# Down products of a two-layer encoder's feed-forward blocks by seven block products in place of eight, and their exchange issued by GpSimd, on one Trainium2 core

## The chip, the cores and the metric

The kernel runs on one core of one Trainium2 chip. The metric is the device time of one execution in microseconds, the median of three runs. All arithmetic is in float32, at the accuracy of float32: each operand is split into a high part (a cast to the type fp32r) and a low part (what the cast left), and a product takes three matmuls (high by high, high by low, low by high).

## The reference

Input `x` is 256 rows of 1024. Two layers; each adds half a feed-forward block (FFN), then a token mixer (retention in layer 0, latent attention in layer 1) together with a cross-attention into memory, then half a second FFN. What the change touches is the FFN:

```python
def swiglu(h, w_gu, w_down):            # w_gu 1024 x 5632, w_down 2816 x 1024
    g, u = jnp.split(h @ w_gu, 2, axis=-1)
    return (jax.nn.silu(g) * u) @ w_down
...
x = x + 0.5 * rms_norm(swiglu(rms_norm(x, ng[0]), ffn_w_gu[l, 0], ffn_w_down[l, 0]), ng[1])
```

There are four of them, named (l, j) here: (0,0), (0,1), (1,0), (1,1).

## The kernel before

The 256 rows are two tiles t of 128. The 2816 hidden columns go in eleven chunks c of 256 (`FC`, `NFC`; `C` is 10). For a chunk and a tile `gu(t, c)` multiplies the normed rows (`zh`, `zl`, columns on partitions) with 8 blocks of gate and up weights side by side: 8 x 3 = 24 matmuls of 512 columns into one PSUM bank. `swiglu` (L311, L313) drains that bank: ScalarE makes s, the silu of the gate half, VectorE multiplies the up half with it into `a`. For the down product the hidden columns must lie on the partitions. `turn` (L330) has VectorE transpose `a` in 32 x 32 squares into `aT`; every two chunks `exchange` moves the squares between partition groups into `ag`: four blocks stay in their partitions and are copied by GpSimd (L265), twelve are moved by DMAs of 32 x 256 (L260), which SP issues. `take` splits `ag` into `ah` and `al`. The last chunk goes through TensorE's transposes instead (`tr`).

`down(t, c)` multiplies a tile's 128 x 256 with the chunk's 256 x 1024: two halves i of 512 columns, two blocks b, three matmuls each, 12 in all, into two banks `accs[t]`; `both(c)` does the two tiles, 24. In the loop the order on TensorE, which is written out by hand, is gu(0, c), gu(1, c), both(c - 3): 72 matmuls of 512 columns. The four accumulators hold four of the eight banks, the rest are for gate/up and transposes.

Weights come by SP's DMAs into `raw` (5 buffers). ScalarE casts the high part `wh` (L75), VectorE subtracts it for the low part `wl` (L76), both in pieces of 1024 columns, with 9 buffers each: four pieces for gate/up and two for down a chunk. The other engines' order is the scheduler's, by the order of the program and by `issue_after`; SP's exchange transfers stand between weight loads in steps (`between`, `moved`). `extra` is other work placed into an FFN's turns: rotary tables, and the memory's preparation for the next mixer. `post` scales the FFN's result, adds it to x, and `pre` prepares the next stage; rsqrt is GpSimd's (L159).

Of the kernel before, what the change touches and what calls it, by code (L numbers as in the profile page):

```python
# [10 lines left out]
F32 = mybir.dt.float32  # L11
# [7 lines left out]
P = 128  # L19
# [3 lines left out]
FC = 256  # L23
# [8 lines left out]
def kernel(ctx, tc, x, mem, positions, norm_gains, ffn_w_gu, ffn_w_down, w_o,  # L32
# [46 lines left out]
    def load_raw(src, cols):  # L79
        with behind(*moved):  # L80
            return load_now(src, cols)

    def load_now(src, cols):
# [10 lines left out]
        if between:  # L94
            between[0][0] -= 1
            if between[0][0] < 0:
                with behind_weights():
                    moved[:] = [between[0][1].pop(0)()]
                if not between[0][1]:
                    between.pop(0)  # L100
# [3 lines left out]
    between, moved = [], []  # L104
# [123 lines left out]
    def post(t, accs, gain, half, next_gain, hook=None):  # L228
# [5 lines left out]
        ends = next_gain is None  # L234
        if not ends:
            scaled(0)
            scaled(1)
# [18 lines left out]
    def exchange(b, g, skip, n):  # L256


        def move(i, q):
            return nc.sync.dma_start(out=g[q * 32:(q + 1) * 32, i * 256:(i + 1) * 256],  # L260
                                     in_=b[i * 32:(i + 1) * 32, q * 256:(q + 1) * 256]).ins
        pairs = []
        for i in range(4):
            sl = slice(i * 32, (i + 1) * 32)
            G.tensor_copy(out=g[sl, i * 256:(i + 1) * 256], in_=b[sl, i * 256:(i + 1) * 256])  # L265
            pairs += [(i, q) for q in range(4) if q != i]
        steps = [lambda p=pairs[k:k + n]: [move(*x) for x in p][-1] for k in range(0, 12, n)]
        if n == 12:
            steps[0]()
        else:  # L270
            between.append([skip, steps])
# [6 lines left out]
    def ffn(l, j, zs, gains, extra=(), first=None):  # L278
        wgu, wd = ffn_w_gu[l, j], ffn_w_down[l, j]
        gu_w, d_w, act, at, pair = {}, {}, {}, {}, {}  # L280
        accs = [[None, None], [None, None]]
        extra = dict(extra)
# [25 lines left out]
        def swiglu(t, c):  # L308
# [4 lines left out]
            a_ins = V.scalar_tensor_tensor(out=a, in0=p[:, FC:2 * FC], scalar=z.r, in1=s,  # L313
                                           op0=ALU.mult, op1=ALU.mult).ins
# [9 lines left out]
        def turn(t, c):  # L324
# [938 lines left out]
```

## Time and profile before

| | before |
|---|---|
| time, median of 3 runs | 963.52 us (962.76 to 964.04) |
| the profiled execution, its own time | 961.57 us |
| its span, first to last instruction | 959.8 us |
| busy: TensorE, VectorE, ScalarE, GpSimd | 947.4, 627.1, 516.7, 78.3 us |
| instructions | 13112 |
| DMA moved | 188.96 MB, 197 GB/s over the span |

The span is of one profiled execution; the time of an execution is 1.8 us longer than its span. Busy time counts the instructions' own durations, and neighbours on an engine overlap a little, so an engine's step from one start to the next can be shorter than its instruction.

### The profile page before, as it was taken

What the parts mean: (1) busy time and instruction counts of PE and PEld (TensorE: products, weight loads), DVE (VectorE), ACT (ScalarE), POOL (GpSimd) and SP (SyncE); (2) the same over time, 40 slices, a digit from 0 to 9 for tenths busy, and PEclk for the clock granted to TensorE, in tenths of its full rate; (3) what the DMA queues carried; (4) which work ended last, traced back from release to release, by engine and by line L of the source; (5) the groups of instructions that cost most, each with busy time, mean ns of one, the idle gap of its engine ahead of it and who ended that gap; (6) DMA issues with size and microseconds to landing.
All of it is one profiled execution on the core that took longest, in us unless ns stands there. A gap on an engine that the chain in (4) does not pass through costs nothing.

```text
span 959.8 us, 13112 instructions
## 1 busy us (share of the span) xinstructions
PE 947.4 (99%) x4503; PEld 788.6 (82%) x4503; DVE 627.1 (65%) x1000; ACT 516.7 (54%) x873; POOL 78.3 (8%) x122
## 2 busy tenths in 40 slices
PE   8999999999999999999999999999999999999997
PEld 7778888898888888888887888888897888878885
DVE  6587657677886846665668456676766884557562
ACT  7455555466655635454546444554658763345451
POOL 0011001020000201000001000001020010100010
PEclk9999999999999999999999999999999999999999
DMA  9488867483745437686745676687551645656851
GB/s 296 126 289 268 254 191 247 151 295 110 211 162 163 132 104 255 198 260 197 249 153 180 209 229 216 210 287 228 169 169 45 220 132 180 198 193 204 271 177 44
DMA packets 148692, 188.96 MB, mean 197 GB/s; under 512 B 13321, under 2 KB 131089, under 8 KB 148625
## 3 DMA queue, kind: packets, MB, share of 16 engines
q1 hardware_dynamic: 148608, 188.12, 60.7%
q8 instruction: 35, 0.57, 0.2%
q14 instruction: 33, 0.26, 0.1%
q10 hardware_dynamic: 16, 0.00, 0.0%
HBM read 179.16 MB, written 1.05 MB: 188 GB/s over the span
## 4 chain that ended last, share of the span: by engine, by line
PE 79%; DMA 6%; SPq 5%; DVE 5%; issue 2%; ACT 2%; POOL 0%; DVEq 0%; POOLq 0%; ACTq 0%
PE bank L156 25%; PE bank L155 25%; PE bank L154 25%; DMA raw<-in_ffn_w_gu_dram 5%; PE bank L184 3%; SPq L91 2%; DVE wl L76 2%; SPq L260 2%; ACT wh L75 1%; PE bank L540 1%; PE bank L572 1%; PE bank L792 1%; PE bank L778 1%; DVE x L248 0%; DVE a L313 0%
## 5 line engine op out<-in xcount | busy, mean ns | idle before, releaser
L76 DVE TENSOR_TENSOR wl<-raw,wh 128x1024 fp32r<-128x1024 f32 (+1 forms) x320 | 383.6, 1213 | 197.3 <-ACT wh L75 193.9
L75 ACT CAST wh<-raw 128x1024 fp32r<-128x1024 f32 (+1 forms) x320 | 331.6, 1047 | 274.0 <-DMA raw<-in_ffn_w_down_dram 109.2
L154 PE MATMUL bank<-wh,zh 128*128 128x512 f32 (+2 forms) x944 | 364.4, 386 | 0.0
L155 PE MATMUL bank<-wl,zh 128*128 128x512 f32 (+2 forms) x944 | 360.7, 382 | 1.3 <-DVE wl L76 1.2
L156 PE MATMUL bank<-wh,zl 128*128 128x512 f32 (+2 forms) x944 | 360.7, 382 | 0.4 <-DVE zl L76 0.4
L155 PEld LDWEIGHTS bank<-wl,zh 128*128 128x128 f32 x944 | 177.7, 188 | 35.4 <-DVE wl L76 2.0
L156 PEld LDWEIGHTS bank<-wh,zl 128*128 128x128 f32 x944 | 177.5, 188 | 34.9 <-DVE zl L76 1.0
L154 PEld LDWEIGHTS bank<-wh,zh 128*128 128x128 f32 x944 | 177.6, 188 | 33.5 <-issue 0.7
L156 PE MATMUL bank<-wh,al 128*128 128x512 f32 x352 | 137.8, 391 | 1.2 <-DVE al L76 1.2
L154 PE MATMUL bank<-wh,ah 128*128 128x512 f32 x352 | 138.2, 393 | 0.1
L155 PE MATMUL bank<-wl,ah 128*128 128x512 f32 x352 | 137.2, 390 | 0.0
L265 POOL COPY ag<-aT 32x256 f32<-32x256 f32 x80 | 40.4, 505 | 501.6 <-DVE aT L330 422.2
L156 PEld LDWEIGHTS bank<-wh,al 128*128 128x128 f32 x352 | 66.1, 188 | 16.8 <-DVE al L76 3.1
L154 PEld LDWEIGHTS bank<-wh,ah 128*128 128x128 f32 x352 | 66.1, 188 | 13.7 <-ACT ah L75 0.5
L155 PEld LDWEIGHTS bank<-wl,ah 128*128 128x128 f32 x352 | 66.1, 188 | 13.4
L311 ACT ACTIVATE s<-bank,rstd 128x256 f32<-128x256 f32 x88 | 41.3, 469 | 51.3 <-PE bank L156 48.4
L313 DVE SCALAR_TENSOR_TENSOR a<-bank,rstd,s 128x256 f32<-128x256 f32 x88 | 42.1, 478 | 32.0 <-ACT s L311 31.7
L168 ACT ACTIVATE junk<-bank 128x512 bf16<-128x512 f32 x24 | 14.4, 599 | 43.0 <-DVE y L233 30.6
L330 DVE STREAM_TRANSPOSE aT<-a 128x256 f32<-128x256 f32 x80 | 35.3, 441 | 1.5
L76 DVE TENSOR_TENSOR al<-ag,ah 128x256 fp32r<-128x256 f32 x80 | 29.7, 417 | 5.7 <-ACT ah L75 5.7
L75 ACT CAST zh<-bank 128x512 fp32r<-128x512 f32 (+2 forms) x54 | 23.0, 455 | 17.6 <-PE bank L184 10.4
L233 DVE TENSOR_TENSOR y<-bank,gpost 128x512 f32<-128x512 f32 x24 | 16.2, 685 | 23.6 <-PE bank L156 19.5
(159 smaller groups left out, 551.2 us busy)
## 6 DMA issues: line engine op xcount, KB each, us to landing
raw<-in_ffn_w_gu_dram SPq DMA_DIRECT2D x352, 256.0 KB, 4.5
raw<-in_ffn_w_down_dram SPq DMA_DIRECT2D x88, 512.0 KB, 4.6
raw<-in_ret_w_in_dram SPq DMA_DIRECT2D x48, 256.0 KB, 4.0
raw<-in_w_o_dram SPq DMA_DIRECT2D x16, 512.0 KB, 4.5
ag<-aT SPq DMA_DIRECT2D x240, 32.0 KB, 2.3
raw<-in_mem_w_kv_dram SPq DMA_DIRECT2D x8, 512.0 KB, 5.3
gpost<-in_norm_gains_dram SPq DMA_DIRECT2D x6, 512.0 KB, 5.9
gpre<-in_norm_gains_dram SPq DMA_DIRECT2D x5, 512.0 KB, 6.3
```

The source lines that it names most:

```text
L75: ins = S.copy(out=hi, in_=src).ins
L76: V.tensor_tensor(out=lo, in0=src, in1=hi.bitcast(F32), op=ALU.subtract)
L91: last_load[0] = nc.sync.dma_start(out=dst[:, k], in_=src[:, k]).ins
L154: T.matmul(out=dst, lhsT=ah, rhs=bh, start=start, stop=False)
L155: T.matmul(out=dst, lhsT=ah, rhs=bl, start=False, stop=False)
L156: T.matmul(out=dst, lhsT=al, rhs=bh, start=False, stop=stop)
L184: T.transpose(out=tp[:s.shape[1], j * P:(j + 1) * P], in_=s, identity=ident)
L260: return nc.sync.dma_start(out=g[q * 32:(q + 1) * 32, i * 256:(i + 1) * 256], in_=b[i * 32:(i + 1) * 32, q * 256:(q + 1) * 256]).ins
L265: G.tensor_copy(out=g[sl, i * 256:(i + 1) * 256], in_=b[sl, i * 256:(i + 1) * 256])
L311: s_ins = S.activation(out=s, in_=p[:, 0:FC], func=AF.Silu, scale=z.r).ins
L313: a_ins = V.scalar_tensor_tensor(out=a, in0=p[:, FC:2 * FC], scalar=z.r, in1=s, op0=ALU.mult, op1=ALU.mult).ins
L330: V.transpose(out=b.rearrange("p (q u t b x) -> p u t q b x", q=4, u=2, t=2, b=2)[:, c % 2, t], in_=act.pop((t, c)).rearrange("p (b q x) - ...
```

## The change

A chunk's down product over both tiles is a 256 x 256 by 256 x 1024 product, seen as 2 x 2 blocks: tile by hidden block b, and hidden block b by column half i. In the first `fast` chunks of an FFN it is made by the Strassen-Winograd form: seven block products of sums and differences in place of eight, each of three matmuls as before. `fast` is 5 in (0,0) and (1,0), and 8 in (0,1) and (1,1).

- Weights (`load_fast`): three blocks x, T's and y's sources come into a tile `wB` and the fourth into `w21`; VectorE makes y (1024 columns), T (512) and w21 (512) as differences between splits.
- Activations (`take_fast`): four sums of 128 columns, and splits of 256, 128 and 512 columns in place of two of 256.
- Order on TensorE: `half(c - 4, 1)`, ten matmuls, behind gu(0, c), and `half(c - 3, 0)`, eleven, behind gu(1, c). The seven products (`prod`) accumulate over the fast chunks in seven banks, which leaves one for gate/up.
- The drain: in these turns ScalarE makes s and also u, the scaled up half; VectorE multiplies the two.
- After chunk fast - 1 `combine` adds the products up; three banks go on as accumulators, and `post` adds the four `sums` to them (two additions of 512 columns for a tile).
- Exchange: GpSimd issues the twelve DMAs, then makes its four copies; the code that put them between SP's loads is gone.
- Tables move to behind gu(1, 1) and gu(1, 2), the memory's steps from turns 6, 7, 8 to 7, 8, 9; one buffer more of `t2`, one fewer of `k1`.

```diff
+        if sums[0] is not None:
+            for a, b in zip(accs, sums):
+                V.tensor_tensor(out=b, in0=a, in1=b, op=ALU.add)
+            accs = sums
...
-    def exchange(b, g, skip, n):
-
-
-        def move(i, q):
-            return nc.sync.dma_start(out=g[q * 32:(q + 1) * 32, i * 256:(i + 1) * 256],
-                                     in_=b[i * 32:(i + 1) * 32, q * 256:(q + 1) * 256]).ins
-        pairs = []
+    def exchange(b, g):
+        for i in range(4):
+            sl = slice(i * 32, (i + 1) * 32)
+            for q in range(4):
+                if q != i:
+                    G.dma_start(out=g[q * 32:(q + 1) * 32, i * 256:(i + 1) * 256], in_=b[sl, q * 256:(q + 1) * 256])
         for i in range(4):
             sl = slice(i * 32, (i + 1) * 32)
             G.tensor_copy(out=g[sl, i * 256:(i + 1) * 256], in_=b[sl, i * 256:(i + 1) * 256])
-            pairs += [(i, q) for q in range(4) if q != i]
-        steps = [lambda p=pairs[k:k + n]: [move(*x) for x in p][-1] for k in range(0, 12, n)]
-        if n == 12:
-            steps[0]()
-        else:
-            between.append([skip, steps])
...
+        def load_fast(c):
+            w = wk.tile([P, 1536], F32, name="wB", tag="A", bufs=2)
+            w21 = esm("wB21")
+            nc.sync.dma_start(out=w[:, 0:1024], in_=block(c, 0, 0, 2))
+            nc.sync.dma_start(out=w[:, 1024:1536], in_=block(c, 1, 1))
+            last_load[0] = nc.sync.dma_start(out=w21, in_=block(c, 1, 0)).ins
+            three = w.rearrange("p (a n) -> p a n", a=3)
+            xh, xl, yh, yl, vh, vl = (wp.tile([P, 1024], F32R, name=n, tag=n)
+                                      for n in ("wh", "wl", "wh", "wl", "wh", "wl"))
+            th, tl = (wk.tile([P, 512], F32R, name=n, tag="e", bufs=5) for n in ("wTh", "wTl"))
+            lo, hi = slice(0, 512), slice(512, 1024)
+            two = lambda a: a.rearrange("p (a n) -> p a n", a=2)
+            split(three[:, 0:3:2], two(xh), two(xl))
+            V.tensor_tensor(out=w[:, 0:1024], in0=w[:, 512:1536], in1=w[:, 0:1024], op=ALU.subtract)
+            split(w[:, 0:1024], yh, yl)
+            split(w21, vh[:, lo], vl[:, lo])
+            V.tensor_tensor(out=three[:, 2], in0=three[:, 2], in1=three[:, 0], op=ALU.subtract)
+            split(three[:, 2], th, tl)
+            V.tensor_tensor(out=w21, in0=w21, in1=three[:, 2], op=ALU.subtract)
+            split(w21, vh[:, hi], vl[:, hi])
+            d_w[c] = [(xh[:, lo], xl[:, lo]), (xh[:, hi], xl[:, hi]), (yh[:, lo], yl[:, lo]), (yh[:, hi], yl[:, hi]),
+                      (vh[:, lo], vl[:, lo]), (vh[:, hi], vl[:, hi]), (th, tl)]
+        def take_fast(c):
+            g = pair.pop(c)
+            A = [[g.rearrange("p (i u t b x) -> p u t b i x", i=4, u=2, t=2, b=2)[:, c % 2, t, b]
+                  for b in range(2)] for t in range(2)]
+            q = lambda a, k, n=1: a[:, k * P:(k + n) * P].rearrange("p (i x) -> p i x", i=4)
+            ah, al = t2("ah", 512, F32R), t2("al", 512, F32R)
+            sr, sh, sl = t2("sr"), t2("sh", 512, F32R), t2("sl", 512, F32R)
+            V.tensor_tensor(out=q(sr, 0), in0=A[1][0], in1=A[1][1], op=ALU.add)
+            V.tensor_tensor(out=q(sr, 1), in0=q(sr, 0), in1=A[0][0], op=ALU.subtract)
+            V.tensor_tensor(out=q(sr, 2), in0=A[0][0], in1=A[1][0], op=ALU.subtract)
+            V.tensor_tensor(out=q(sr, 3), in0=A[0][1], in1=q(sr, 1), op=ALU.subtract)
+            split(g.rearrange("p (i u t b x) -> p u t b i x", i=4, u=2, t=2, b=2)[:, c % 2, 0],
+                  ah[:, 0:FC].rearrange("p (b i x) -> p b i x", i=4, b=2),
+                  al[:, 0:FC].rearrange("p (b i x) -> p b i x", i=4, b=2))
+            split(A[1][1], q(ah, 2), q(al, 2))
+            split(sr, sh, sl)
+            n = lambda k: slice(k * P, (k + 1) * P)
+            a = lambda k: (ah[:, n(k)], al[:, n(k)])
+            z = lambda k: (sh[:, n(k)], sl[:, n(k)])
+            at[c] = [a(0), z(3), z(0), z(2), a(1), a(2), z(1)]
+        def down_fast(c, *ms):
+            if c not in d_w:
+                load_fast(c)
+            if c == 0 and 0 in ms:
+                prod.extend(bank() for _ in range(7))
+                accs[0][:] = prod[4], prod[1]
+                accs[1][0] = prod[5]
+            for m in ms:
+                p, x = divmod(m, 3)
+                (ah, al), (bh, bl) = at[c][p], d_w[c][p]
+                own = p in (1, 4, 5)
+                T.matmul(out=prod[p], lhsT=al if x == 2 else ah, rhs=bl if x == 1 else bh,
+                         start=c == 0 and x == 0, stop=x == 2 and c == fast - 1 and not own)
+        def combine():
+            m1, m5, m7, m6 = prod[0], prod[2], prod[3], prod[6]
+            c1, u, v, w = esm("c1"), esm("u"), esm("v"), esm("w")
+            S.copy(out=c1, in_=m1)
+            add = lambda o, a, b: V.tensor_tensor(out=o, in0=a, in1=b, op=ALU.add)
+            add(u, m6, c1)
+            add(v, m5, u)
+            add(u, m7, u)
+            add(w, m5, u)
+            sums[:] = [[c1, v], [u, w]]
...
-            a_ins = V.scalar_tensor_tensor(out=a, in0=p[:, FC:2 * FC], scalar=z.r, in1=s,
-                                           op0=ALU.mult, op1=ALU.mult).ins
+            if 3 < c < fast + 4 and (t, c) != (1, C):
+                u = k1("u")
+                s_ins = S.activation(out=u, in_=p[:, FC:2 * FC], func=AF.Copy, scale=z.r).ins
+                a_ins = V.tensor_tensor(out=a, in0=u, in1=s, op=ALU.mult).ins
+            else:
+                a_ins = V.scalar_tensor_tensor(out=a, in0=p[:, FC:2 * FC], scalar=z.r, in1=s,
+                                               op0=ALU.mult, op1=ALU.mult).ins
...
+        def half(c, h):
+            if 0 <= c < fast:
+                down_fast(c, *(range(11, 21) if h else range(11)))
+                if h and c == fast - 1:
+                    combine()
...
         for c in range(3, C):
             gu(0, c)
+            half(c - 4, 1)
             gu(1, c)
...
-            both(c - 3)
+            if c - 3 < fast:
+                half(c - 3, 0)
+            else:
+                both(c - 3)
         gu(0, C)
-        both(C - 3)
+        half(C - 4, 1)
+        if C - 3 < fast:
+            half(C - 3, 0)
+            half(C - 3, 1)
+        else:
+            both(C - 3)
...
-    zs = ffn(0, 1, zs, lambda: (gpost(0, 5), gpre(1, 0)))
+    zs = ffn(0, 1, zs, lambda: (gpost(0, 5), gpre(1, 0)), fast=8)
```

TensorE, FFN (0,1), with the change: the ten matmuls of a chunk's second half between two runs of 24 gate/up matmuls (zh, zl are the normed rows; ah, al the activations; sh, sl their sums; wTh, wTl the parts of T).

```order
L144 MATMUL bank<-wh,zl 128x512
L342 MATMUL bank<-wh,sl 128x512
L342 MATMUL bank<-wh,ah 128x512
L342 MATMUL bank<-wl,ah 128x512
L342 MATMUL bank<-wh,al 128x512
L342 MATMUL bank<-wh,ah 128x512
L342 MATMUL bank<-wl,ah 128x512
L342 MATMUL bank<-wh,al 128x512
L342 MATMUL bank<-wTh,sh 128x512
L342 MATMUL bank<-wTl,sh 128x512
L342 MATMUL bank<-wTh,sl 128x512
L142 MATMUL bank<-wh,zh 128x512
```

Before, gate/up of both tiles came without a break, and then the 24 down matmuls in one run; now eleven and ten stand behind one tile's gate/up each.

VectorE, FFN (0,1), before: what stands between the transposes of two tiles in the loop.

```order
L330 STREAM_TRANSPOSE aT<-a 128x4x64
L76 TENSOR_TENSOR wl<-raw,wh 128x1024 x6
L313 SCALAR_TENSOR_TENSOR a<-bank,rstd,s 128x256
L76 TENSOR_TENSOR al<-ag,ah 128x256 x2
L330 STREAM_TRANSPOSE aT<-a 128x4x64
```

The same place with the change.

```order
L76 TENSOR_TENSOR wl<-wB,wh 128x1024
L382 TENSOR_TENSOR a<-u,s 128x256
L297 TENSOR_TENSOR wB<-wB 128x1024
L401 STREAM_TRANSPOSE aT<-a 128x4x64
L300 TENSOR_TENSOR wB<-wB 128x512
L76 TENSOR_TENSOR wl<-wB,wh 128x1024
L76 TENSOR_TENSOR wl<-wB_4194,wh 128x512
L76 TENSOR_TENSOR wTl<-wB,wTh 128x512
L302 TENSOR_TENSOR wB_4194<-wB_4194,wB 128x512
L76 TENSOR_TENSOR wl<-wB_4194,wh 128x512
L382 TENSOR_TENSOR a<-u,s 128x256
L315 TENSOR_TENSOR sr<-ag 128x128
```

The subtractions for y, T and w21 stand between the splits that wait for ScalarE's casts of their results, and `a` no longer reads the bank.

GpSimd with the change: the exchanges of one FFN's loop (five in each FFN).

```order
L254 DMA ag<-aT 32x256 x12
L257 COPY ag<-aT 32x256 x4
L254 DMA ag<-aT 32x256 x12
L257 COPY ag<-aT 32x256 x4
L254 DMA ag<-aT 32x256 x12
```

Before, SP's queue held the transfers in twos between its loads, as `L260 DMA ag<-aT 32x256 x2`, and GpSimd held the copies alone.

## Rows read from the trace of the kernel before

**Rows 1.** The page, part 1: busy time, share of the span, instructions, by engine.

```profile
PE 947.4 (99%) x4503; PEld 788.6 (82%) x4503; DVE 627.1 (65%) x1000; ACT 516.7 (54%) x873; POOL 78.3 (8%) x122
```

**Rows 2.** The page, part 2: TensorE's busy tenths and granted clock in 40 slices.

```profile
PE   8999999999999999999999999999999999999997
...
PEclk9999999999999999999999999999999999999999
```

**Rows 3.** The page, part 4: the chain that ended last, by engine.

```profile
PE 79%; DMA 6%; SPq 5%; DVE 5%; issue 2%; ACT 2%; POOL 0%; DVEq 0%; POOLq 0%; ACTq 0%
```

**Rows 4.** Timeline of TensorE, FFN (0,1): start us, us of one, what.

```profile
437.37 0.39 PE L154 MATMUL bank<-wh,zh 128*128 128x512 f32 x1
...
444.85 0.39 PE L154 MATMUL bank<-wh,zh 128*128 128x512 f32 x1
```

**Rows 5.** Groups of instructions by form: xcount | busy us, mean ns of one | idle before.

```profile
L76 DVE TENSOR_TENSOR wl<-raw,wh 128x1024 fp32r<-128x1024 f32 x312 | 376.8, 1222 | 195.7 <-ACT wh L75 192.3
L75 ACT CAST wh<-raw 128x1024 fp32r<-128x1024 f32 x312 | 325.6, 1053 | 269.6 <-DMA raw<-in_ffn_w_down_dram 109.2 <-DMA raw<-in_ffn_w_gu_dram 98.8 <-PE bank L156 23.9
L313 DVE SCALAR_TENSOR_TENSOR a<-bank,rstd,s 128x256 f32<-128x256 f32 x88 | 42.1, 478 | 32.0 <-ACT s L311 31.7
L311 ACT ACTIVATE s<-bank,rstd 128x256 f32<-128x256 f32 x88 | 41.3, 469 | 51.3 <-PE bank L156 48.4 <-POOL rstd L159 2.9
L265 POOL COPY ag<-aT 32x256 f32<-32x256 f32 x80 | 40.4, 505 | 501.6 <-DVE aT L330 422.2 <-DVE ms L172 31.0 <-DMA gpre<-in_norm_gains_dram 23.4
L330 DVE STREAM_TRANSPOSE aT<-a 128x256 f32<-128x256 f32 x80 | 35.3, 441 | 1.5
L76 DVE TENSOR_TENSOR al<-ag,ah 128x256 fp32r<-128x256 f32 x80 | 29.7, 417 | 5.7 <-ACT ah L75 5.7
...
L208 DVE TENSOR_TENSOR z<-x,gpre 128x512 f32<-128x512 f32 x20 | 12.9, 685 | 0.0
...
L159 POOL TENSOR_TENSOR prs<-ms,nhalf 128x1 f32<-128x1 f32 x12 | 9.8, 814 | 203.2 <-DVE ms L172 203.2
...
L76 DVE TENSOR_TENSOR zl<-bank,zh 128x128 fp32r<-128x128 f32 x20 | 5.7, 285 | 2.1 <-ACT zh L75 2.1
```

**Rows 6.** Timeline of VectorE: instructions of one kind back to back.

```profile
202.43 4.62 DVE L76 TENSOR_TENSOR wl<-raw,wh 128x1024 fp32r<-128x1024 f32 x4
...
461.93 0.75 DVE L76 TENSOR_TENSOR al<-ag,ah 128x256 fp32r<-128x256 f32 x2
...
496.51 1.29 DVE L208 TENSOR_TENSOR z<-x,gpre 128x512 f32<-128x512 f32 x2
```

**Rows 7.** Timeline of two drains: last gate/up matmul, then ScalarE's s.

```profile
431.70 0.39 PE L156 MATMUL bank<-wh,zl 128*128 128x512 f32 x1
...
432.49 0.47 ACT L311 ACTIVATE s<-bank,rstd 128x256 f32<-128x256 f32 x1
...
632.04 0.39 PE L156 MATMUL bank<-wh,zl 128*128 128x512 f32 x1
...
637.29 0.47 ACT L311 ACTIVATE s<-bank,rstd 128x256 f32<-128x256 f32 x1
```

**Rows 8.** Waits of ScalarE for gate/up: us in total, times, longest us.

```profile
ACT s L311 <- PE bank L156: 48.4, 22, 5.0
```

**Rows 9.** The exchange's tile ag: duration ns min/median/max; time from issue to landing.

```profile
L260 SPq DMA_DIRECT2D ag<-aT x240: 507/589/1552, 35.9 to 926.1; - x120
L265 POOL COPY ag<-aT x80: 386/393/1479, 36.0 to 921.1; 32x256 f32<-32x256 f32 x80
...
DMA to landing us min/median/max: 1.8/2.3/4.2
```

**Rows 10.** Timeline of GpSimd: one small operation beside a VectorE train, one alone.

```profile
202.60 4.87 POOL L159 TENSOR_TENSOR rstd<-ms,nhalf 128x1 f32<-128x1 f32 x1 [2.80 <-DVE ms L172]
...
212.96 0.55 POOL L159 TENSOR_TENSOR rstd<-ms,nhalf 128x1 f32<-128x1 f32 x1 [5.50 <-DVE ms L172]
```

**Rows 11.** Timeline at FFN (0,1)'s end: the wait that the extra sums lengthen.

```profile
510.50 0.50 PE L155 MATMUL bank<-wl,zh 128*128 128x512 f32 x1 [0.59 <-DVE wl L76]
```

More of the change, by code (lines that the diff above doesn't have):

```diff
@@ L226, in pre, with post @@
         return z
-    def post(t, accs, gain, half, next_gain, hook=None):
+    def post(t, accs, gain, half, next_gain, hook=None, sums=(None, None)):
         y = [t2("y") for i in range(2)]
@@ L276, in gu_src, with ffn @@
                 .rearrange("(k p) (h f) -> p k h f", p=P, h=2)[:, :, :, c * FC:(c + 1) * FC])
-    def ffn(l, j, zs, gains, extra=(), first=None):
+    def ffn(l, j, zs, gains, extra=(), first=None, fast=0):
         wgu, wd = ffn_w_gu[l, j], ffn_w_down[l, j]
@@ L281, in ffn @@
         accs = [[None, None], [None, None]]
+        sums, prod = [[None, None], [None, None]], []
         extra = dict(extra)
@@ L343, in take @@
         def take(c):
-            assert not between, between
+            if c < fast:
+                return take_fast(c)
             g = pair.pop(c)
@@ L371, in down @@
                     mm3(accs[t][i], ah[:, m], al[:, m], wh[:, n], wl[:, n],
-                        c == 0 and b == 0, c == NFC - 1 and b == 1)
+                        new and b == 0, c == NFC - 1 and b == 1)
         def both(c):
@@ L394, in ffn @@
         gu(1, 1)
+        if 1 in extra:
+            with behind_weights():
+                extra[1]()
         gu(0, 2)
         gu(1, 2)
+        if 2 in extra:
+            with behind_weights():
+                extra[2]()
         for c in range(3, C):
             gu(0, c)
+            half(c - 4, 1)
             gu(1, c)
@@ L415, in ffn @@
         with in_order():
-            z0 = post(0, accs[0], gain_post, True, next_gain, lambda: swiglu(1, C))
+            z0 = post(0, accs[0], gain_post, True, next_gain, lambda: swiglu(1, C), sums[0])
         down(1, C - 2)
@@ L423, in ffn @@
         down(1, C, (1,))
-        z1 = post(1, accs[1], gain_post, True, next_gain)
+        z1 = post(1, accs[1], gain_post, True, next_gain, None, sums[1])
         norm_behind(z0)
@@ L1218, in third @@
             m.put(1)
-        return {6: first, 7: second, 8: third}
+        return {7: first, 8: second, 9: third}
     m0 = Mem(0)
-    zs = ffn(0, 0, zs, lambda: (gpost(0, 1), gpre(0, 2)), {3: tables, 4: tables2, **mem_extra(m0)}, first=First())
+    zs = ffn(0, 0, zs, lambda: (gpost(0, 1), gpre(0, 2)), {1: tables, 2: tables2, **mem_extra(m0)}, first=First(), fast=5)
     zs = retention(zs, m0, lambda: (gpost(0, 3), gpre(0, 4)))
-    zs = ffn(0, 1, zs, lambda: (gpost(0, 5), gpre(1, 0)))
+    zs = ffn(0, 1, zs, lambda: (gpost(0, 5), gpre(1, 0)), fast=8)
     m1 = Mem(1)
-    zs = ffn(1, 0, zs, lambda: (gpost(1, 1), gpre(1, 2)), mem_extra(m1))
+    zs = ffn(1, 0, zs, lambda: (gpost(1, 1), gpre(1, 2)), mem_extra(m1), fast=5)
     zs = mla(zs, m1, lambda: (gpost(1, 3), gpre(1, 4)))
-    ffn(1, 1, zs, lambda: (gpost(1, 5), None))
+    ffn(1, 1, zs, lambda: (gpost(1, 5), None), fast=8)
 _INS = ['x', 'mem', 'positions', 'norm_gains', 'ffn_w_gu', 'ffn_w_down', 'w_o', 'mem_norm', 'mem_w_kv',
```

23 lines of the change are left out of this document (7 added, 16 removed).

## Prediction

> **What bounds the kernel now.** I read the page first. TensorE is busy 99% of the span, VectorE 65%, ScalarE 54%, GpSimd 8% [rows 1], and the slices show TensorE at 9 tenths or more everywhere but at the two ends, with its clock at full speed throughout (2.4 GHz) [rows 2]. In the chain of waits 79% is TensorE's own work, 5% each is VectorE, SP's queue and 6% DMA [rows 3]; those are mostly the weight preparation that runs ahead, not stops of TensorE. So time leaves this kernel by removing matmuls, and comes back wherever another engine then stops TensorE. The timeline gives the price of a matmul: from 437.37 to 444.85 lie 33 of them, 0.2267 us each [rows 4]. Its row says 0.39, but they overlap; the step counts.
>
> A measurement can tell about 0.2% (1.9 us) from no change. The sum is made against the profiled execution, 961.57, which is 1.95 below the median of 963.52; I add 1.95 at the end.
>
> **What is removed.** A chunk's down product falls from 24 to 21 matmuls in 5 + 8 + 5 + 8 = 26 chunks: 78 x 0.2267 = **-17.7 us**. All of it lies on the path. A loop turn for one chunk goes from 72 to 69 matmuls: 16.32 to 15.64 us. SP loses 240 issues of the exchange at 0.589 us [rows 9]; SP's queue otherwise only issues loads, which run ahead, so this is costed at nothing; if a load does come earlier, ScalarE's cast comes earlier, and TensorE, which is not waiting for it, gains nothing.
>
> **VectorE in a fast chunk.** Per chunk it now has seven operations of 1024 columns (four gate/up splits, x, the subtraction for y, y), six of 512 (two halves of v, T's subtraction and split, w21's subtraction, the split of the sums), three of 256 (al and two products a), five of 128 and two transposes. Two prices bound it. By the means of [rows 5] (1.222, 0.685, 0.417, 0.285, 0.441; the 512 from the z row, the 128 from zl, a from al): 8.55 + 4.11 + 1.25 + 1.43 + 0.88 = 16.2 us. Back to back an instruction steps faster than it lasts: four of 1024 take 4.62, so a step is (4.62 - 1.22) / 3 = 1.13; two of 512 take 1.29, a step of 0.605; two of 256 take 0.75, a step of 0.333 [rows 6]; taking 0.08 off the others likewise gives 0.21 and 0.36. By steps: 7.93 + 3.63 + 1.00 + 1.05 + 0.72 = 14.3 us. Two GpSimd copies of the exchange fall into each chunk, 0.393 each [rows 9]; if VectorE stands still for them, that is 0.8 more: 15.1 to 17.0. TensorE's chunk is 15.64, so the excess is between nothing and 1.4 us a chunk, 0 to 36 us over 26. A saturated engine goes by steps, but it also waits for ScalarE: the y, T and v splits each need a cast between two of its operations. ScalarE itself has six casts of 1024 (1.053), six smaller ones and four drains of 0.47 [rows 5], about 11.4 us, so it has room, but stands in order behind VectorE's subtractions. I take 15.9, nearer to the steps: 0.25 x 26 = **+6.5 us**.
>
> **The single bank.** Seven product banks leave one for gate/up. Each must be drained within the 10 or 11 matmuls of a half: 11 steps (2.49) less 0.39 for the last matmul to end, less s and u (0.47 each, [rows 5]) leaves some 1.2 us by which ScalarE may come late. Before, it came 0.4 us after the end in one case (431.70 to 432.49) and 4.9 in another (632.04 to 637.29) [rows 7], and TensorE had spare banks. Only 22 of 88 times did ScalarE stand waiting for the bank [rows 8]; in the others it was busy or held. Reading up by ScalarE's u takes VectorE out of the drain. The lower bound is nothing. The upper: if one drain in five of the 52 came 4.9 late, 10 x 3.7 = 37 us. I take nothing beyond the 6.5, because a drain is late here through the same queue of splits that the 15.9 already carries, and count one cost for both. The four drains of (1,3), which still go through VectorE, come in the first half with one bank: s, then a, 0.95 with a wait between; 0.4 each, **+1.6**.
>
> **The exchange.** GpSimd now issues twelve transfers and only then makes its four copies. No row shows a transfer issued there. Below stands SP's issue of the same transfer, 0.589; above, the longest of the copies, 1.48 [rows 9]; the middle is 1.04, and a small GpSimd operation, prs, has a mean of 0.81 [rows 5]. By 1.04 it takes 12.5, then 2.3 to land: about 15 us. In the loop an exchange has 104 matmuls (23.6 us) before it is taken, the first of an FFN 72 (16.3): both covered. The last, in the FFNs with fast 8, has some 18.1 us from the last gate/up of chunk 9 to chunk 8's down product and needs about 3 + 14.8 + 0.4 = 18.2; I give it 0.5 each, **+1.0**. With fast 5 it is covered. If ag is late, ScalarE stands in the cast ah with the next drain queued behind it, so TensorE stops for the bank too. On GpSimd's queue the twelve stand ahead of nothing but copies and, at an FFN's end, the norm's prs, which comes well after the last of them. The bounds are 0 (0.589) and 2 x 5.4 = 11 us (1.48).
>
> **What only moves.** The rotary tables go from turns 3 and 4 to behind chunks 1 and 2, where there are no down products to prepare yet; the memory's three steps go one turn later, so that two of three fall behind most of the fast chunks. Their instructions stay the same: 0, and if VectorE is bound in those turns, their price is inside the excess above.
>
> **The ends.** Each tile's two sums are two additions of 512 columns ahead of the norm, 0.605 + 0.685. Where FFN (0,1) passes to (1,0) TensorE already stands for VectorE there, 0.59 us [rows 11]: **+1.3**. At the kernel's end the first addition lies beside the last six matmuls and the second delays the square: **+0.7**. At the other two ends the next transposes come several microseconds after the halves of z are there, so 0 there.
>
> Sum: -17.7 + 6.5 + 1.6 + 1.0 + 1.3 + 0.7 = **-6.6**; profile 955.0, median **957.0**.
>
> **A rule that speaks against it.** A GpSimd rstd lasted 4.87 us beside four back-to-back splits of VectorE, and 0.55 beside none [rows 10]: GpSimd does stand still for VectorE. The Trainium skill, "SBUF — State Buffer", section on who interferes with whom, says that a transfer issued by GpSimd needs descriptors written by GpSimd, starved while VectorE holds the shared port, and advises SP or ScalarE as issuer; for VectorE instructions with two SBUF inputs it restricts the lock to GpSimd instructions that read. The rstd reads, and agrees; no row shows what an issue does.
>
> **Rivals.**
> *All of it hidden.* VectorE goes by steps, drains are in time: -17.7 + 4.6 = -13.1, median 950.4; without the ends' costs 945.8. For it: the 14.3 us. Against: the 4.9 us drain, and the casts between its operations.
> *VectorE becomes the bound (the other side).* Place: the fast chunks, in the train of split, subtract, split. Price: at 16.6 us a chunk, between 15.9 and 17.0, (16.6 - 15.64) x 26 = 25; -17.7 + 25 + 4.6 = +12, median 975.5. It decides from (17.7 - 4.6) / 26 = 0.50 us of excess, 16.14 us a chunk, only 0.24 above what I took. For it: the mean durations, the copies that hold it up, and drains queued behind it.
> *Near break-even.* An excess of 0.43 to 0.58 gives 961.6 to 965.5.
> *GpSimd's issues are held.* If each stood half a VectorE step longer (0.57), the twelve take 19.3 and land at 22 us: still inside 23.6 in the loop, but 5 us late for each first pair and 6 us for each last exchange, some 4 x 5 + 2 x 6 = 32 us if nothing absorbed it, half of it if the next gate/up did: 957 + 16 to 32, 973 to 989. For it: [rows 10]. Against: the copies' median of 0.393 in a program with VectorE at 65%.
> That the change does not remove its matmuls I give no chance: the order of TensorE's instructions shows 11 and 10 in the halves.
>
> **How the numbers follow.** Forecast (952 to 961.5) 0.41; all hidden (945 to 952) 0.20; near break-even 0.12; VectorE bound (965.5 to 977) 0.19; issues held 0.08. Faster by over 0.2% takes the first two and a piece of break-even: 0.62. Same 0.09, slower 0.29. The range holds most of all but the last: 946 to 976. The likeliest case's own range is 952 to 961.5.
>
> **What would show it.** TensorE's matmuls 78 fewer, 929.7 us of steps in place of 947.4. VectorE busy well above 627, with hardly any idle time in the fast chunks. In the windows of a fast chunk 69 matmuls in 15.6 to 16.2 us. If TensorE waits there, I expect the wait for VectorE's split or for the bank drained by ScalarE's u. GpSimd's twelve issues should span 8 to 15 us, and ah should wait for ag only in the last exchange. The prediction is wrong if the chunks take over 16.14 us, if the twelve issues span over 17 us, or if the drains stop TensorE by over a microsecond in more than a few chunks.

## The result and the profile after

The changed kernel takes 950.44 us (median of 4 runs, 949.74 to 951.24) against 963.14 of the kernel before in the same session; the ratio is 0.9874, 95% interval 0.9855 to 0.9893. That is 12.7 us less, where 6.5 were forecast as likeliest: inside the range, on the forecast side, and in size the rival "all of it hidden" (950.4). The profiled execution took 950.34, with a span of 948.5, 11.3 less than before.

From the page of the changed kernel: busy time by engine, the slices of VectorE, and the chain.

```profile
PE 930.7 (98%) x4425; PEld 773.5 (82%) x4425; DVE 782.7 (83%) x1318; ACT 587.6 (62%) x1027; POOL 226.1 (24%) x362
...
DVE  5899968587886778999988899876676888999995
...
PE 81%; DMA 6%; DVE 5%; ACT 3%; issue 3%; POOL 1%; SPq 1%; DVEq 0%; POOLq 0%; ACTq 0%
```

Beside [rows 1], TensorE has 78 matmuls fewer and VectorE 156 us more: it now shows 9 tenths through the fast loops. GpSimd's 226 us holds 118 us of issuing, which it did not do before.

The windows of the fast loops, changed kernel (from:to, length, then busy us and instructions of TensorE, its weight loads, VectorE, ScalarE, GpSimd; clock, DMA share, GB/s): four chunks of FFN (1,0), and six each of (0,1) and (1,1).

```profile
367.93:461.77 93.84, 93.84 (x415) 77.70 (x414) 89.19 (x139) 62.13 (x95) 30.75 (x48) 1.00 0.67 209
545.91:608.47 62.56, 62.56 (x277) 51.82 (x276) 59.42 (x93) 40.27 (x62) 20.14 (x32) 1.00 0.58 178
810.08:903.92 93.84, 93.84 (x416) 77.70 (x414) 89.24 (x139) 62.24 (x95) 30.47 (x48) 1.00 0.63 201
```

Six chunks in 93.84 us are 15.64 each, exactly 69 steps of 0.2267: TensorE is not stopped once. VectorE needs 89.19 / 6 = 14.87 of the 15.64: near the steps (14.3), and under the 15.1 that I had with VectorE standing still for the copies.

One drain in that loop, changed kernel's timeline: the last gate/up matmul, and ScalarE's s and u.

```profile
391.28 0.39 PE L144 MATMUL bank<-wh,zl 128*128 128x512 f32 x1
...
391.70 0.47 ACT L377 ACTIVATE s<-bank,rstd 128x256 f32<-128x256 f32 x1 [0.48 <-PE bank L144]
392.08 0.47 ACT L381 ACTIVATE u<-bank,rstd 128x256 f32<-128x256 f32 x1
```

ScalarE stands waiting for the bank (0.48 us) and starts 0.03 us after the matmul ends (391.67); the bank is free at 392.55, 0.88 us after, of the 2.1 there are. In the loops of FFN (0,1) and (1,1) no drain starts over 0.1 us after its last matmul; the latest of (0,0)'s starts 2.6 us late, at 57.0, beside the stops of the first down product shown below. ScalarE's waits show what is gone, changed kernel (us, times, longest):

```profile
ACT s L377 <- PE bank L144: 45.9, 53, 4.1
...
ACT wh L75 <- DMA raw<-in_ffn_w_gu_dram: 27.5, 19, 4.0
...
ACT wh L75 <- DMA raw<-in_ffn_w_down_dram: 4.1, 5, 1.5
```

Before, it waited 98.8 and 109.2 us for the FFN's weights to land [rows 5], with the drains queued behind those casts, and for the bank only 22 times [rows 8]. The late drain of [rows 7], at 637.29, stood behind two such casts; the kernel before, ScalarE's timeline:

```profile
633.63 1.05 ACT L75 CAST wh<-raw 128x1024 fp32r<-128x1024 f32 x1 [1.58 <-DMA raw<-in_ffn_w_gu_dram]
636.33 1.05 ACT L75 CAST wh<-raw 128x1024 fp32r<-128x1024 f32 x1 [1.66 <-DMA raw<-in_ffn_w_gu_dram]
```

Now the weights are there, and it waits for TensorE.

TensorE's stops that are new or longer, from its timeline in the changed kernel (the bracket is the idle time and what ended it; the step lost is up to 0.3 us more).

```profile
24.51 0.50 PE L142 MATMUL bank<-wh,zh 128*128 128x512 f32 x1 [0.56 <-ACT wh L75]
25.77 0.50 PE L143 MATMUL bank<-wl,zh 128*128 128x512 f32 x1 [0.76 <-DVE wl L76]
...
55.86 0.50 PE L342 MATMUL bank<-wh,al 128*128 128x512 f32 x1 [1.01 <-DVE al L76]
57.80 0.50 PE L342 MATMUL bank<-wh,sl 128*128 128x512 f32 x1 [0.89 <-DVE sl L76]
...
136.42 0.30 PE L172 MATMUL bank<-ident,m 128*128 128x128 f32 x1 [0.92 <-DVE m L573]
137.59 0.33 PE L172 MATMUL bank<-ident,m 128*128 128x128 f32 x1 [0.54 <-DVE u L350]
...
506.86 0.50 PE L143 MATMUL bank<-wl,zh 128*128 128x512 f32 x1 [1.11 <-DVE wl L76]
...
624.85 0.30 PE L172 MATMUL bank<-ident,m 128*128 128x128 f32 x1 [0.58 <-DVE m L573]
626.02 0.33 PE L172 MATMUL bank<-ident,m 128*128 128x128 f32 x1 [0.55 <-DVE u L350]
```

They lie at the edges: the first weights of FFN (0,0), its first down product, the memory's transposes after `combine` in (0,0) and (1,0), and the passage that [rows 11] showed.

At the first down product the exchange has landed: ScalarE casts ah without waiting. VectorE reaches its splits late, al at 55.41 and sl at 57.08, behind weight splits and the four sums (54.27 to 55.47).

At the memory's transposes TensorE waits for the normed m, and m for its rstd, which GpSimd makes. The sum of squares is ready at 129.27, but GpSimd is busy with the exchange: it issues until 133.11, then copies, and only then comes to rstd (in (1,0): ready at 618.19, rstd at 623.36). `combine`'s first addition, u, stands behind m in VectorE's queue, and with it the bank for the second transposes. Lines of the changed kernel for both places:

```profile
52.94 0.60 ACT L75 CAST ah<-ag 128x256 fp32r<-128x256 f32 x2
...
133.15 1.69 POOL L257 COPY ag<-aT 32x256 f32<-32x256 f32 x4
134.93 0.56 POOL L147 TENSOR_TENSOR rstd<-ms,nhalf 128x1 f32<-128x1 f32 x1
...
135.53 1.41 DVE L573 SCALAR_TENSOR_TENSOR m<-m,rstd,raw 128x512 f32<-128x512 f32 x2 [2.47 <-POOL rstd L147]
```

Counting each matmul that starts more than 0.12 us later than one step (0.2267) behind the one before it, TensorE lost 8.1 us before and 12.9 now. The end, from the last matmul's start to the end of the span, went from 959.8 - 953.2 = 6.6 to 948.5 - 940.9 = 7.6. So -17.7 + 4.8 + 1.0 = -11.9 of the span's -11.3; the remaining 0.6 is not in the count.

The exchange's tile in the changed kernel (duration ns min/median/max; time from issue to landing):

```profile
L254 POOL DMA_DIRECT2D ag<-aT x240: 496/496/667, 38.6 to 914.0; - x120
L257 POOL COPY ag<-aT x80: 386/767/1428, 47.7 to 917.5; 32x256 f32<-32x256 f32 x80
...
DMA to landing us min/median/max: 1.6/2.6/6.7
```

An issue takes 0.496 us, under SP's 0.589 [rows 9], and at most 0.667 beside a VectorE busy 95% of the time. The copies, which read, doubled at the median (0.393 to 0.767). The twelve issues of an exchange span 5.9 to 9.1 us.

### The profile page after: what moved, and what is told of

It reads as the page before. It is cut to its first block, busy times and chain, and to the rows that moved or that the text cites. A ratio compares the mean times of both kernels' runs of the same rounds, so it can differ in the third digit from the quotient of the medians.

```text
span 948.5 us, 13719 instructions
## 1 busy us (share of the span) xinstructions
PE 930.7 (98%) x4425; PEld 773.5 (82%) x4425; DVE 782.7 (83%) x1318; ACT 587.6 (62%) x1027; POOL 226.1 (24%) x362
## 3 DMA queue, kind: packets, MB, share of 16 engines
HBM read 179.16 MB, written 1.05 MB: 190 GB/s over the span
## 4 chain that ended last, share of the span: by engine, by line
PE 81%; DMA 6%; DVE 5%; ACT 3%; issue 3%; POOL 1%; SPq 1%; DVEq 0%; POOLq 0%; ACTq 0%
PE bank L144 22%; PE bank L142 22%; PE bank L143 22%; PE bank L342 12%; PE bank L172 2%; DMA raw<-in_ffn_w_gu_dram 2%; DVE wl L76 2%; DMA ag<-aT 2%; ACT wh L75 1%; DMA wB<-in_ffn_w_down_dram 1%; PE bank L632 1%; DMA m<-in_mem_dram 1%; PE bank L884 1%; PE bank L870 1%; ACT e L643 0%
## 5 line engine op out<-in xcount | busy, mean ns | idle before, releaser
L76 DVE TENSOR_TENSOR wl<-raw,wh 128x1024 fp32r<-128x1024 f32 (+1 forms) x268 | 322.9, 1230 | 38.5 <-ACT wh L75 37.1
L75 ACT CAST wh<-raw 128x1024 fp32r<-128x1024 f32 (+1 forms) x268 | 276.3, 1045 | 82.6 <-DMA raw<-in_ffn_w_gu_dram 27.5
L254 POOL DMA_DIRECT2D ag<-aT x240 | 118.1, 499 | 359.2 <-ACT sh L75 212.2
L75 ACT CAST wh<-wB 128x1024 fp32r<-128x1024 f32 (+1 forms) x104 | 84.7, 836 | 69.8 <-DVE wB L297 39.9
L76 DVE TENSOR_TENSOR wl<-wB,wh 128x1024 fp32r<-128x1024 f32 (+1 forms) x104 | 98.4, 966 | 9.8 <-ACT wh L75 9.7
L257 POOL COPY ag<-aT 32x256 f32<-32x256 f32 x80 | 67.4, 843 | 3.1
L142 PE MATMUL bank<-wh,ah 128*128 128x512 f32 x144 | 57.1, 396 | 0.0
L144 PE MATMUL bank<-wh,al 128*128 128x512 f32 x144 | 56.2, 390 | 0.0
L143 PE MATMUL bank<-wl,ah 128*128 128x512 f32 x144 | 56.1, 389 | 0.0
L147 POOL TENSOR_TENSOR rstd<-ms,nhalf 128x1 f32<-128x1 f32 x16 | 24.2, 1512 | 85.6 <-DVE ms L160 85.4
L384 DVE SCALAR_TENSOR_TENSOR a<-bank,rstd,s 128x256 f32<-128x256 f32 x42 | 20.1, 478 | 16.5 <-ACT s L377 16.5
```

Of the source, the lines that this page charges most:

```text
L75: ins = S.copy(out=hi, in_=src).ins
L76: V.tensor_tensor(out=lo, in0=src, in1=hi.bitcast(F32), op=ALU.subtract)
L142: T.matmul(out=dst, lhsT=ah, rhs=bh, start=start, stop=False)
L143: T.matmul(out=dst, lhsT=ah, rhs=bl, start=False, stop=False)
L144: T.matmul(out=dst, lhsT=al, rhs=bh, start=False, stop=stop)
L147: G.tensor_tensor(out=dst, in0=src, in1=nhalf.broadcast_to(list(src.shape)), op=ALU.pow)
```

## The experiments

Ratios are to the kernel before in the same session; the changed kernel's own is 0.9874 [0.9855, 0.9893].

**No block products.** `fast=0` in the four calls; all else of the change stays.

```diff
-... fast=5)  ... fast=8)
+...)         ...)
```

> The changed kernel with fast 0 in all four FFNs: no block products, everything else of the change stays (GpSimd issues the exchange, tables and memory steps moved). Theory: the 78 matmuls are the whole gain, 17.7 us, and what the blocks give back (the memory's transposes that wait for combine, 3.2 us, and the sums at the ends, 1.2 us) goes with them: 950.4 + 17.7 - 4.4 = 963.7, level with the kernel before (961.5 to 966). Rival: the issuer or the moved work gives part of the gain: then clearly below the kernel before, 955 to 960.

959.05 us, ratio 0.9962 [0.9946, 0.9978]: the rival's side. 0.2 to 0.5% of the time, some 2 to 5 us of the gain, have nothing to do with the block products. Its span is 957.5, so the blocks are worth 9.0 us by the spans, of 17.7 in matmuls. The lost part of before that is gone here is five stops of TensorE in the FFNs, 2.7 us together: at a late weight and the first exchange of (0,0), and at the second exchange of (0,1) and of (1,1), each behind a cast of ScalarE that waited 1.6 to 7.5 us for weights. One of them in the kernel before:

```profile
849.88 0.50 PE L156 MATMUL bank<-wh,al 128*128 128x512 f32 x1 [0.59 <-DVE al L76]
```

**No block products, and SP issues the exchange in one batch.** To part the issuer from the moment of issue.

```diff
-                    G.dma_start(out=g[...], in_=b[...])
+                    nc.sync.dma_start(out=g[...], in_=b[...])
```

> As e1_no_blocks (no block products), but SP issues the twelve transfers in one batch. e1 came out 4.1 us under the kernel before, where I had expected none; its trace shows 2.6 us of stops fewer, all at the first exchange or at a late weight of an FFN. Theory: what helped is that the transfers go out at once and not in steps between loads: 958 to 960.5 here too. Rival: it is the issuer, since SP's loads no longer stand behind the wait for aT: 961.5 to 966.

961.98 us, ratio 0.9995 [0.9978, 1.0012]: the rival; its interval just touches that of GpSimd as issuer, and the ratios are 0.33% apart, 3.2 us. Only the issuer differs between the two. With SP the loads stand behind the exchange: in the first one SP issues the twelve transfers from 36.98 to 44.56 us, and the next weight load at 44.61. TensorE stops for 3.44 us at the first down product, where the cast of ah stands behind three casts that waited for weights, and ScalarE waits 79.5 us for the FFN's weights, with GpSimd as issuer 23.1. The drains go with it: the one below starts 5.4 us after its last matmul (387.40), while with GpSimd as issuer none in the loops of (0,1), (1,0) and (1,1) is over 0.1 us late. (The profiled execution here, 964.28, is one of the two longest of ten.) From the timeline of this kernel, its waits, and the waits of the one with GpSimd:

```profile
55.26 0.50 PE L142 MATMUL bank<-wh,ah 128*128 128x512 f32 x1 [3.44 <-ACT ah L75]
...
390.57 1.05 ACT L75 CAST wh<-raw 128x1024 fp32r<-128x1024 f32 x1 [6.17 <-DMA raw<-in_ffn_w_down_dram]
...
392.79 0.46 ACT L377 ACTIVATE s<-bank,rstd 128x256 f32<-128x256 f32 x1
...
ACT wh L75 <- DMA raw<-in_ffn_w_gu_dram: 43.9, 33, 4.5
ACT wh L75 <- DMA raw<-in_ffn_w_down_dram: 35.6, 22, 6.2
```

```profile
ACT wh L75 <- DMA raw<-in_ffn_w_gu_dram: 22.0, 13, 3.9
...
ACT wh L75 <- DMA raw<-in_ffn_w_down_dram: 1.1, 1, 1.1
```

**SP issues the exchange in the changed kernel.** The same edit with the blocks kept.

> The changed kernel with the exchange's twelve transfers issued by SP in one batch, GpSimd keeping its four copies. Theory: transfers are covered by the matmuls between, and SP's loads run ahead: 950.4 within 1.5 us. Rival: SP's queue stands at the first transfer until aT is there and then takes 12 x 0.589 = 7.1 us, so that the weights behind it come late and a VectorE with 0.8 us of room a chunk cannot catch up: 956 to 975.

951.85 us, ratio 0.9900 [0.9870, 0.9930]: within the theory. By the medians it is 1.4 us above the changed kernel, but the intervals overlap widely, so a gain of the issuer beside the blocks is not shown, and one of 1 to 3 us not excluded. The rival's 956 to 975 is out. ScalarE waits no longer for the FFN's weights than with GpSimd as issuer (20.1 us beside 31.6), and a drain of the loop starts 0.04 us after its last matmul. From this kernel's waits and timeline:

```profile
ACT wh L75 <- DMA raw<-in_ffn_w_gu_dram: 17.6, 19, 2.5
...
ACT wh L75 <- DMA raw<-in_ffn_w_down_dram: 2.5, 4, 1.7
...
392.85 0.47 ACT L377 ACTIVATE s<-bank,rstd 128x256 f32<-128x256 f32 x1 [0.46 <-PE bank L144]
```

So in the kernel with the blocks the early drains do not come from the issuer. SP has its own price here: three of m's four loads stand behind the twelve (124.40 to 131.94, m at 132.03), and the stops at the memory's transposes are 1.36 and 1.91 us, for 0.92 and 0.58 with GpSimd.

**A second subtraction in each fast chunk,** of 1024 columns, then two of them.

```diff
             split(w[:, 0:1024], yh, yl)
+            V.tensor_tensor(out=yl, in0=w[:, 0:1024], in1=yh.bitcast(F32), op=ALU.subtract)
```

> One more VectorE operation of 1024 columns in each of the 26 fast chunks (yl is computed a second time). VectorE is busy 89.2 of 93.84 us in six fast chunks, 14.9 of 15.64 a chunk. Theory: its idle 0.77 us can be used and nothing more: a step of 1.13 gives an excess of 0.36 x 26 = 9 us, 956 to 963. Rival, the edge is already reached (the idle time is waits that stay): 26 x 1.13 = 29 us, 975 to 982. Rival, there is more room, since preparation runs ahead into the turns without down products: 950 to 953.

956.26 us, ratio 0.9943 [0.9924, 0.9961]: 5.8 more, at the low end of the theory. The loop of FFN (0,1) still ran at 15.64 (first halves at 368.31 and 383.94), with VectorE full, and 142 of its instructions in the six chunks' window of 93.84 us where the changed kernel had 139, not 145: the deficit was taken from weights split ahead. It came out at the ends of (0,1) and (1,1), in the lines below, and in (0,0) in one drain that stopped TensorE for 1.05 us at 99.33:

```profile
368.00:460.00 92.00, 92.00 (x408) 76.00 (x407) 90.42 (x140) 56.94 (x92) 29.80 (x48) 1.00 0.64 200
```

```profile
477.68 0.50 PE L343 MATMUL bank<-wl,ah 128*128 128x512 f32 x1 [0.98 <-DVE wl L76]
...
921.54 0.50 PE L343 MATMUL bank<-wl,ah 128*128 128x512 f32 x1 [0.58 <-DVE wl L76]
```

> Two more VectorE operations of 1024 columns in each fast chunk. With one, the loop itself still ran at 15.64 us a chunk and the stops came at the FFN's end: the deficit was drawn from weights prepared ahead. Theory: with two, 17.1 us a chunk, the reserve is soon used up and the loop runs at VectorE's pace: excess 1.5 x 26 = 39 us less some 3 us of reserve in each FFN: 970 to 985. Rival: the reserve is large (nine buffers of weights) and holds through five or eight chunks: 960 to 966.

988.91 us in one run, 38 more, a little over the theory. Counted as above, TensorE lost 48.4 us (12.9 in the changed kernel), in FFN (0,1) 3.3 of them in the loop and 9.5 behind it. Among its waits are those for VectorE's splits wl and for the second added subtraction (L300 here):

```profile
PE bank L143 <- DVE wl L76: 18.1, 10, 2.8
...
PE bank L344 <- DVE wl L300: 8.4, 2, 5.0
```

The rival I gave 0.19, VectorE as the bound, is thus real, and it lies between one and two such operations (1.13 and 2.26 us) a chunk away.

**The drain without u.**

```diff
-            if 3 < c < fast + 4 and (t, c) != (1, C):
+            if False:
```

> The changed kernel with u left out: VectorE reads the up half from the bank as before, also in the fast turns. With u the bank is empty 0.88 us after its last matmul, and the next gate/up writes it some 2.1 us after. Theory: s takes 0.5, then at most one VectorE operation of 1.2 us and a of 0.48 stand before it is free: 2.2 at worst, so little is lost: 950 to 954. Rival: a stands behind several operations in VectorE's queue, as in the drains of 4.9 us that I feared: about 1 us in each of 52 drains, 980 to 1005.

949.92 us, ratio 0.9874 [0.9841, 0.9906]: no loss. The loop stays at 15.64 a chunk, so u is not what keeps the drain short. One drain stops TensorE for VectorE's `a`, 0.58 us at 76.28 in FFN (0,0). In windows, six chunks of FFN (0,1):

```profile
367.93:461.77 93.84, 93.84 (x416) 77.73 (x415) 89.93 (x139) 58.43 (x85) 30.52 (x48) 1.00 0.67 209
```

**Tables back in turns 3 and 4.**

```diff
-    ... {1: tables, 2: tables2, **mem_extra(m0)} ...
+    ... {3: tables, 4: tables2, **mem_extra(m0)} ...
```

> The changed kernel with the rotary tables back in turns 3 and 4. Theory: the tables' VectorE work behind chunks 1 and 2 delays the first preparation and the first exchange's sums, which cost 2.1 us at 21 to 26 us and 2.2 us at 56 to 58 us of the span; up to 4 us come back, less what the tables cost in a turn where VectorE has 0.8 us of room and runs ahead by little: 946.5 to 949.5. Rival: those stops belong to the block products' weights and not to the tables: 950 to 952, or more if the tables now stop the fast loop.

952.92 us, ratio 0.9914 [0.9887, 0.9941]: the theory fell. The stops at 24 to 26 us and 55 to 58 us stay (they go with the block products: the kernel without blocks has no stop there), and FFN (0,0)'s loop now stops for the bank. The tables stand in VectorE's queue (until 79.5 for the first), ScalarE's casts wait for VectorE's subtraction, and the drain stands behind the casts; at the second stop the cast waits 2.83 us for it:

```profile
80.81 1.57 ACT L75 CAST wh<-wB 128x1024 fp32r<-128x1024 f32 x2 [2.29 <-DVE wB L297]
...
83.69 0.50 PE L142 MATMUL bank<-wh,zh 128*128 128x512 f32 x1 [0.72 <-ACT u L381]
...
100.53 0.50 PE L142 MATMUL bank<-wh,zh 128*128 128x512 f32 x1 [0.90 <-ACT u L381]
```

That is the single bank's price where a drain is late: 0.9 and 1.1 us of step here, 0.3 and 0.5 in two later turns. It is the coupling of VectorE, casts and drain that the prediction priced for the fast loops. The tables' move, which I costed at nothing ("what only moves"), avoids it; the intervals of the two kernels just overlap.

**The memory's first load a turn earlier.**

```diff
-        return {7: first, 8: second, 9: third}
+        return {6: first, 8: second, 9: third}
```

> The changed kernel with the memory's first load in turn 6 in place of 7 (second and third stay). Theory: the stop of 1.08 and 0.74 us at the memory's transposes is the load of m that lands late; it goes in both FFNs, the 0.59 us each that wait for combine's bank stay: 948.5 to 950. Rival: VectorE's queue is what makes it late, and the norm of m now stands in a turn with little room: 950 to 952.

947.84 us, ratio 0.9860 [0.9832, 0.9887]. That is under the theory's range: in its timeline all four stops at the memory's transposes are gone, also the two for `combine`'s bank, which the theory had kept; with m made earlier, u stands behind it no longer. One late drain comes in FFN (0,0), at 98.87 (0.92 us), behind ScalarE's wait of 1.61 us for m's load. By the intervals it can't be told from the changed kernel; its span is 2.6 us shorter.

**Six fast chunks in (0,0) and (1,0),** and the memory's last two steps a turn later, so that m is loaded two turns ahead.

```diff
-        return {7: first, 8: second, 9: third}
+        return {7: first, 9: second, 10: third}
...
-    ... First(), fast=5)    ... mem_extra(m1), fast=5)
+    ... First(), fast=6)    ... mem_extra(m1), fast=6)
...
+        if C in extra:
+            with behind_weights():
+                extra[C]()
         tr(0, C)
```

> Six in place of five fast chunks in FFN (0,0) and (1,0), the memory's second and third step one turn later (the last behind the down product of chunk 7). Theory: VectorE's room is enough and each fast chunk is worth its three matmuls, 0.68 us: 2 x 0.68 = 1.4 less, and m, loaded two turns ahead, no longer late (1.8): 947 to 949.5. Rival: VectorE's reserve, which the fast chunks use up, is gone one chunk earlier and the end of the FFN stops: 950 to 955.

946.67 us, ratio 0.9848 [0.9823, 0.9872]; its span, 944.1, is 4.4 below the changed kernel's. The fastest seen: it beats the kernel before, and the changed one by the spans, while the intervals just overlap. No stop at the memory's transposes is left. It holds two changes, and the share of each was not taken apart.

**Eight in (1,0)**, the memory's steps at turn 8, behind chunk 7's down product, and ahead of tile 0's last:

```diff
-        return {7: first, 9: second, 10: third}
+        return {8: first, 10: second, 11: third} if late else {7: first, 9: second, 10: third}
...
+        if 11 in extra: ...
         down(0, C)
```

> As e9_fast6, with eight fast chunks in FFN (1,0) too; the memory's steps for layer 1 go to turn 8, behind the down product of chunk 7, and ahead of the last down product of tile 0. Theory: two more fast chunks are worth 1.4 us, and the late third step costs at most its own transposes' wait: 944.5 to 947 beside 946.7. Rival: the memory's splits now stand beside the norm of tile 0 and delay the start of the attention: 947.5 to 951.

953.18 us, ratio 0.9908 [0.9880, 0.9936]: the rival's direction, and worse than it said. It has fewer matmuls than any other, and its span is 7.8 us longer than with six chunks. 7.5 us of it are lost between 640 and 690 us, at the FFN's end, where the version with six stops nowhere: at chunk 7's product, and behind the memory's transposes, which hold the first half of tile 1's last gate/up,

```profile
652.17 0.79 PE L342 MATMUL bank<-wh,sl 128*128 128x512 f32 x1 [1.38 <-DVE sl L76]
...
661.12 0.50 PE L142 MATMUL bank<-wh,zh 128*128 128x512 f32 x1 [1.89 <-DVE zl L76]
```

and in matmuls at the lower clock level after each of the two (granted clock 0.55 from 652.2 to 656.0 us, 0.66 from 661.0 to 666.0). The rival's cause, the memory's splits, is in the second stop (zl), at the FFN's end and not at the attention's start; why VectorE, busy 9.52 of the 10 us to 650, is late with sl at the first was not taken apart.

**The space for GpSimd's descriptors,** `dynamic_dma_scratch_size` 512 and 1536 in place of 1024.

> The space for GpSimd's transfer descriptors halved (512 for 1024 bytes a partition). In several exchanges of the changed kernel GpSimd issued eight transfers back to back and the ninth waited for one of them to land. Theory: that is the space, and now it issues four and then waits; twelve take some 3 landings of 2.6, up to 10 us, which the 15.6 us turns still cover, so the time stays within 2 us of 950.4 but for the last exchanges. Rival: the wait for the landing has another cause, and eight still go out back to back.

> The same space at 1536 bytes in place of 1024. Theory of the space: all twelve go out back to back in some 6 us in every exchange; the time stays at 950.4 within 2 us, as the exchange is covered. Rival: the ninth still waits in some exchanges.

949.91 and 950.74 us, one run each. The theory of the space fell: with half of it GpSimd still issues eight back to back, and then waits for a landing,

```profile
349.46 4.09 POOL L254 DMA_DIRECT2D ag<-aT  x8 [13.93 <-DVE aT L401]
356.13 2.21 POOL L254 DMA_DIRECT2D ag<-aT  x4 [2.57 <-DMA ag<-aT]
```

in other exchanges twelve go out in 6 us, and with one and a half times the space the ninth waits as often: over 0.3 us in 6 of 20 exchanges, in the changed kernel and in both of these. What holds it stays open; the exchange is covered either way.

## Why the prediction was right in range and wrong in its likeliest case

**The matmuls, -17.7:** right. 78 fewer, a chunk 15.64.

**VectorE and the drains, +6.5:** this is the step that failed. The loops lost nothing. I set 15.9 because an engine with dependences on ScalarE would not go by steps; it took 14.87, near the steps, and with one operation more, at 16.0, the loops of all FFNs but (0,0) still kept 15.64, as VectorE had run ahead. My edge of 16.14 was about right: at 14.87 + 1.13 = 16.0 the kernel lost 5.8, and at 17.1 it was far behind the kernel before. I left the upper bound of the drains at 37 us from the row 632.04 [rows 7] without asking why ScalarE was late there: it stood at casts that waited for weights (633.63 and 636.33, above), and that wait was about to go.

**SP's 240 issues, 0:** wrong. I wrote that TensorE was not waiting for the loads. It was, at five places in the FFNs, 2.7 us; and ScalarE waited 208 us for them. Without block products, taking the transfers off SP's queue is worth 3 us, with the issuer as the cause: the two kernels without blocks show it, and with SP the drains there are up to 5.4 us late. With the blocks SP as issuer leaves the weights as early and the drains as short, so the early drains of the changed kernel need another cause. The transfers' batch alone is not it (the kernel without blocks and with SP has it, and late drains). What is left is what came with the blocks, as the down weights' own buffers; that was not tried and stays open.

**The four drains of (1,3), +1.6:** nothing. No stop stands there in any of the four FFNs.

**The exchange, +1.0:** an issue takes 0.496, below the lower bound I took from SP, and the last exchanges are in time: ah does wait for ag there, as forecast (2.2 to 4.3 us in the four FFNs), but TensorE does not stop. The first of FFN (0,0) is in time too: the stops of 1.01 and 0.89 us at the first down product are VectorE's splits, late behind weights and sums. What I missed is on GpSimd's queue: I wrote that the twelve stand ahead of nothing but copies and an FFN's end's prs, but the memory's rstd stands there too.

**The ends, +1.3 and +0.7:** 1.11 - 0.59 = 0.5 of idle time at the passage, and 1.0 at the kernel's end.

**Not in the sum:** 2.1 us of steps at the first weights of FFN (0,0) and 3.0 at the memory's transposes. The first goes with the blocks (it is absent without them, and stays with the tables moved back). The second is one chain: m's load lands while GpSimd is in the exchange, rstd waits in its queue, m waits for rstd, and `combine` stands behind m; all four stops went when the load was moved. It belongs to "what only moves", which I put at nothing.

So the blocks' own costs were not far from my 11.1: 17.7 - 9.0 = 8.7 by the spans. They lie elsewhere than I put them, and 2 to 3 us that the kernel without blocks already gains came on top (its span is 2.3 us under the one before). That the rival "all of it hidden" gave the measured time is partly chance: it hid the right term, kept 4.6 of others that came out differently, and knew nothing of the gain without blocks nor of the memory's 3.0.

**The rule that spoke against it.** The Trainium skill, "SBUF — State Buffer", section on who interferes with whom, warns of a GpSimd issuer starved while VectorE holds the shared port in its 2-port mode, and of VectorE instructions with two SBUF inputs, which most of the added work here is, it says that only a GpSimd instruction that reads is locked out. With the second the trace agrees: an issue never took over 0.667 us with VectorE at 95%, while the copies went from 0.393 to 0.767. The advised issuer, SP, was no faster with blocks and 3 us slower without.

## What to carry to other kernels

Before a queue's instructions are priced at nothing, look at who waits for what stands behind them: without the blocks SP's transfers held the weight loads, the loads held ScalarE's casts, and the casts held the drains, and on GpSimd's queue the same transfers held the memory's norm. An engine that prepares ahead can run at 95% without stopping the one it feeds; when it was overloaded here, most of the deficit showed at the end of a stage and not in the loop. When accumulators take all banks but one, whatever makes the draining engine wait in those turns can stop TensorE, here for 0.3 to 1.2 us each; put it where the banks are free.

## What the runs showed of the hardware that was not expected

TensorE's clock fell after a short stop in one kernel and did not after a like stop in another. In the changed kernel with SP as issuer it stood 0.90 us at 57 us, and then the granted clock was 0.52 (the lower level, 1.2 GHz) for three microseconds; the changed kernel itself stood 0.89 us at the same place and kept full speed. Windows of the kernel with SP as issuer:

```profile
52.00:57.00 5.00, 3.67 (x15) 2.35 (x13) 5.00 (x12) 4.08 (x8) 0.00 (x0) 1.00 0.99 316
57.30:58.30 1.00, 1.00 (x4) 0.87 (x5) 1.00 (x2) 0.09 (x1) 0.00 (x0) 0.87 1.09 382
58.40:61.60 3.20, 3.20 (x9) 2.45 (x8) 3.20 (x10) 0.62 (x1) 0.97 (x1) 0.52 1.09 391
```

and of the changed kernel, the same stretch:

```profile
57.90:61.60 3.70, 3.70 (x17) 3.05 (x18) 3.70 (x10) 0.66 (x2) 0.00 (x0) 1.00 0.83 257
```

Nine matmuls in 3.2 us against seventeen in 3.7: a stop of a microsecond can cost more behind it, or nothing. What decides it these runs do not show.
